# Decoder trunk on one core: the low parts of 40 weight chunks, made by an accumulating DMA instead of a GpSimd subtraction

## The chip, the cores and the metric

The kernel runs on one core of one Trainium2 chip. The metric is device time in microseconds (us), the median of several runs. The profile is one execution taken with the hardware profiler. Engines: PE (TensorE matmuls), PEld (TensorE weight loads), DVE (VectorE), ACT (ScalarE), POOL (GpSimd), SP (SyncE, which issues nearly all DMAs here).

## What is computed

The reference is a decoder trunk of two layers over 512 tokens of width 1024, in float32:

```
for l in range(DEPTH):
    h = rmsnorm(x, attn_norm_w[l])
    proj = h @ w_in[l]                      # split into the inputs of three mixers
    ... y_ssd = ssd_mixer(...); y_sc = short convolution; y_nsa = nsa_mixer(...)
    x = x + concatenate([y_ssd, y_sc, y_nsa]) @ w_out[l]
    h = rmsnorm(x, ffn_norm_w[l])
    u = causal_dwconv(h @ ffn_w_up[l], ffn_conv_w[l], ffn_conv_b[l])
    gate, val = split(u, 2)
    x = x + (silu(gate) * val) @ ffn_w_down[l]
return rmsnorm(x, final_norm_w)
```

## The kernel before, in words

**Products in three parts.** Weights and activations are float32. Each is split into a high part, rounded to the type fp32r, and a low part, the rest. A product is three matmuls into the same PSUM tile (`mul3`, L195 to L200): high weight by high activation (L198), high weight by low activation (L199), low weight by high activation (L200). So the low part of a weight chunk is wanted first by the third matmul of that chunk.

**Weight chunks.** The weights come in chunks of 128x1024 float32 (512 KB), listed in `chunks` (L108 to L128) in the order of their use, each with the engine that makes its low part, V (DVE) or G (POOL). Per layer there are the group chunks, 22 chunks of the input projection mixed with four compression chunks (`w0` to `w3`), 8 of the output projection, and then those of the MLP. G makes 20 whole chunks per layer, 40 in all: 15 of the input projection (q1, xbc2 to xbc7, z0, z2, z3, sc0, sc1, sc3 to sc5) and 5 of the output projection. It also makes two of the compression chunks of a layer, on another path (L172). All chunks of the MLP go to V.

**Staging.** `do_dma` (L132) loads a chunk from HBM into a `raw` tile on the SP queue (3 buffers). `do_prep` (L150) makes the `hl` tile (4 buffers) that holds both parts: ACT copies raw into the high part (L175), which rounds it, and then the chunk's engine subtracts, low = raw - high (L176). `nxt` (L179), called when a chunk's matmuls begin, sees to it that loads are issued to four chunks ahead and chunks prepared to three ahead. An `hl` buffer comes free when PE is done with the chunk four places earlier; a `raw` buffer comes free when both preparing instructions have read it.

**What lies beside it.** In each layer the first part runs the projection and the mixers together: `pull` (L512) inserts steps of the projection between attention and scan pieces. The pieces pass from engine to engine: `scores` (L604) goes PE, DVE, ACT, then scales the probabilities on DVE and POOL (L624); `turn` (L627) transposes on PE (L632), ACT writes the high part (L636), DVE the low part (L639), and `pv` (L646) multiplies on PE (L652). The scan has POOL work at L754, L796, L813, L816 and L817. `post_xbc` (L367) has DVE (L369), ACT (L371), three DVE steps (L373) and an ACT tanh (L374). `values`, `parts` and `post_keys` make operands with ACT and DVE; L334 and L335 belong to `post_q`. The MLP (`ffn`, L934) has no POOL work.

**What sets the order.** Each engine runs its instructions in order, and that order is fixed when the program is built: the framework places instructions on an engine by its own cost estimates and dependencies, while `keep_in_program_order` pins some matmuls behind what was traced before them. Engines wait for one another by semaphores.

Of the kernel before, what the change touches and what calls it, by code (L numbers as in the profile page):

```python
# [10 lines left out]
F32 = mybir.dt.float32  # L11
F32R = mybir.dt.float32r
AF = mybir.ActivationFunctionType
OP = mybir.AluOpType
# [49 lines left out]
def trunk(ctx: ExitStack, tc: tile.TileContext, ins, out):  # L64
    nc = tc.nc
    V, A, G, TE = nc.vector, nc.scalar, nc.gpsimd, nc.tensor
# [7 lines left out]
    def slot(dt=F32, shape=(P, 512)):  # L74
        return ph.tile(list(shape), dt, tag="s", bufs=32, name="s")
# [74 lines left out]
    def do_prep(i):  # L150
        _, w, eng, piece = chunks[i]
        r = raws.pop(i)
        if w < 0:
            ts_ = []
            for j in range(2):
                t = slot(F32R)
                rr = r[:, j * 512:(j + 1) * 512]
                A.activation(t, rr, AF.Copy)
                V.tensor_tensor(t[64:128], rr[64:128], t[64:128].bitcast(F32), op=OP.subtract)
                ts_.append(t)  # L160
            hls[i] = ts_
            return
        t = pw.tile([P, 2, 1024], F32R, tag="hl", bufs=4, name="hl")
        if piece:

            n, line = w // piece, -(-2 * piece // 16) * 16
            t3 = t.rearrange("p e c -> p (e c)")[:, :n * line].rearrange("p (k c) -> p k c", c=line)[:, :, :2 * piece]
            t4 = t3.rearrange("p k (e c) -> p k e c", e=2)
            r3 = r[:, :w].rearrange("p (k c) -> p k c", c=piece)
            for a, b in ((0, 1), (1, 4)) if i == 0 else ((0, n),):  # L170
                A.activation(t4[:, a:b, 0], r3[:, a:b], AF.Copy)
                eng.tensor_tensor(t4[:, a:b, 1], r3[:, a:b], t4[:, a:b, 0].bitcast(F32), op=OP.subtract)  # L172
            hls[i] = t4
            return
        A.activation(t[:, 0, 0:w], r[:, 0:w], AF.Copy)  # L175
        eng.tensor_tensor(t[:, 1, 0:w], r[:, 0:w], t[:, 0, 0:w].bitcast(F32), op=OP.subtract)  # L176
        hls[i] = t

    def nxt():  # L179
        i = st["use"]  # L180
        st["use"] += 1
        while st["dma"] < min(len(chunks), i + 5):
            do_dma(st["dma"])
            st["dma"] += 1
        while st["prep"] < min(len(chunks), i + 4):
            do_prep(st["prep"])
            st["prep"] += 1
        return hls.pop(i)
# [874 lines left out]
    for k in range(KD):  # L1063
        if k in (0, 3, 6):
            do_prep(st["prep"])
            st["prep"] += 1
        n.split(k)
# [109 lines left out]
```

## Time and profile before

| | us |
|---|---|
| median of 3 runs | 1258.81 (1256.79 to 1263.97) |
| the profiled execution's own time | 1256.38 |
| its span, first to last instruction | 1254.6 |
| PE busy / DVE busy / ACT busy / POOL busy | 1199.0 / 879.5 / 581.3 / 226.5 |
| mean granted TensorE clock | 0.988 |

A row of a profile view names the line of the kernel, the engine, the operation and its tiles as out<-in, with partitions x elements and a type. In a timeline a row is the start in us, the duration, the instruction, how many alike follow one another, and in brackets how long the engine had been idle before it and who ended that. In a table by stretch each engine has its busy time in us and its instructions; then come the granted clock (1 is 2.4 GHz, 0.5 is 1.2 GHz), the busy share of the DMA engines and what they moved.

### The profile page before, as it was taken

How to read it: one execution, taken by the hardware profiler on the slowest of the kernel's cores; microseconds unless marked ns; L12 is line 12 of the kernel's file. 1: busy time of each engine (PE TensorE's matmuls, PEld its weight loads, DVE VectorE, ACT ScalarE, POOL GpSimd, SP SyncE). 2: the span in 40 equal slices, each digit the busy share in tenths (PEclk: the TensorE clock that was granted, in tenths of full speed). 3: DMA queues.
4: the chain of work that ended last, by engine and by line, in shares of the span. 5: the costliest groups of instructions: out<-in, count | busy, mean ns of one | idle time of the engine just before them, and what ended most of it. 6: DMA issues, size and time to landing. Idle time of an engine off the chain costs nothing. (4 is left out here: it accounts for less than half of the span.)

```text
span 1254.6 us, 15502 instructions
## 1 busy us (share of the span) xinstructions
PE 1199.0 (96%) x5843; PEld 994.0 (79%) x5843; DVE 879.5 (70%) x1408; ACT 581.3 (46%) x909; POOL 226.5 (18%) x209
## 2 busy tenths in 40 slices
PE   8889899999999999999999888999999999999997
PEld 6767678788888888888877667778888888888897
DVE  6899978567776347775468998795577743677753
ACT  6655554345443224444348455444444421444553
POOL 3443346500000000000043332562000000000001
PEclk9999999999999999999999998999999999999999
DMA  7321123232322332232223211322232333233452
GB/s 257 117 67 51 51 86 100 75 100 95 101 96 90 101 101 98 89 116 91 80 84 101 68 51 51 121 81 84 89 102 95 101 101 95 91 101 101 127 162 99
DMA packets 37051, 121.33 MB, mean 97 GB/s; under 512 B 4144, under 2 KB 6512, under 8 KB 36976
## 3 DMA queue, kind: packets, MB, share of 16 engines
q1 hardware_dynamic: 36832, 120.33, 30.2%
q8 instruction: 46, 0.75, 0.3%
q14 instruction: 29, 0.24, 0.1%
q10 hardware_dynamic: 144, 0.00, 0.0%
HBM read 118.19 MB, written 2.13 MB: 96 GB/s over the span
## 5 line engine op out<-in xcount | busy, mean ns | idle before, releaser
L198 PE MATMUL mm<-h,hl 128*128 128x512 f32 x1040 | 412.3, 396 | 0.8 <-DVE s L369 0.8
L199 PE MATMUL mm<-h,hl 128*128 128x512 f32 x1040 | 408.8, 393 | 0.0
L200 PE MATMUL mm<-h,hl 128*128 128x512 f32 x1040 | 408.6, 393 | 0.1
L175 ACT ACTIVATE hl<-raw 128x1024 fp32r<-128x1024 f32 x198 | 209.6, 1058 | 225.2 <-PE mm L200 122.5
L176 DVE TENSOR_TENSOR hl<-raw,hl 128x1024 fp32r<-128x1024 f32 x158 | 195.5, 1238 | 104.7 <-ACT hl L175 102.6
L198 PEld LDWEIGHTS mm<-h,hl 128*128 128x128 f32 x1040 | 197.3, 190 | 41.0 <-issue 1.0
L200 PEld LDWEIGHTS mm<-h,hl 128*128 128x128 f32 x1040 | 196.7, 189 | 41.1 <-DVE hl L176 0.5
L199 PEld LDWEIGHTS mm<-h,hl 128*128 128x128 f32 x1040 | 197.1, 190 | 39.3
L212 POOL TENSOR_TENSOR m<-m,mhalf 128x1 f32<-128x1 f32 (+2 forms) x14 | 9.9, 708 | 773.7 <-DVE m L211 773.7
L943 DVE SCALAR_TENSOR_TENSOR s<-s,par 128x511 f32<-128x511 f32 (+1 forms) x172 | 128.3, 748 | 3.5 <-ACT s L941 0.6
L176 POOL TENSOR_TENSOR hl<-raw,hl 128x1024 fp32r<-128x1024 f32 x40 | 98.9, 2476 | 123.6 <-ACT hl L175 86.4
L940 DVE TENSOR_TENSOR s<-mm,rstdB 128x512 f32<-128x512 f32 x86 | 59.1, 689 | 66.7 <-PE mm L200 66.7
L199 PE MATMUL mm<-s,hl 128*128 128x512 f32 (+1 forms) x240 | 85.2, 355 | 3.4 <-DVE s L258 3.4
L198 PE MATMUL mm<-s,hl 128*128 128x512 f32 (+1 forms) x240 | 85.5, 357 | 1.1 <-ACT s L257 1.1
L200 PE MATMUL mm<-s,hl 128*128 128x512 f32 (+1 forms) x240 | 85.0, 354 | 0.0
L257 ACT ACTIVATE s<-s 128x512 fp32r<-128x512 f32 (+1 forms) x62 | 33.0, 545 | 111.8 <-DVE s L958 108.0
L198 PE MATMUL aux<-s,hl 128*128 128x512 f32 (+1 forms) x232 | 82.1, 354 | 0.0
L199 PE MATMUL aux<-s,hl 128*128 128x512 f32 (+1 forms) x232 | 81.8, 353 | 0.0
L200 PE MATMUL aux<-s,hl 128*128 128x512 f32 (+1 forms) x232 | 81.8, 353 | 0.0
L941 ACT ACTIVATE s<-s,par 128x512 f32<-128x512 f32 x86 | 69.3, 808 | 8.8 <-DVE s L940 8.2
L258 DVE TENSOR_TENSOR s<-s 128x512 fp32r<-128x512 f32 (+1 forms) x62 | 45.1, 738 | 27.9 <-ACT s L257 27.9
L956 ACT ACTIVATE s<-s 128x512 f32<-128x512 f32 x40 | 25.3, 633 | 78.7 <-DVE s L943 78.7
(257 smaller groups left out, 1677.6 us busy)
## 6 DMA issues: line engine op xcount, KB each, us to landing
raw<-in_w_up SPq DMA_DIRECT2D x86, 512.0 KB, 3.5
raw<-in_w_dn SPq DMA_DIRECT2D x54, 512.0 KB, 3.5
raw<-in_w_in SPq DMA_DIRECT2D x44, 512.0 KB, 3.6
raw<-in_w_out SPq DMA_DIRECT2D x16, 512.0 KB, 3.5
raw<-in_w SPq DMA_DIRECT2D x8, 512.0 KB, 3.5
s<-dr SPq DMA_DIRECT2D x16, 256.0 KB, 4.2
x<-in_xT SPq DMA_DIRECT2D x8, 256.0 KB, 5.8
out<-s SPq DMA_DIRECT2D x8, 256.0 KB, 3.2
```

The source lines that it names most:

```text
L175: A.activation(t[:, 0, 0:w], r[:, 0:w], AF.Copy)
L176: eng.tensor_tensor(t[:, 1, 0:w], r[:, 0:w], t[:, 0, 0:w].bitcast(F32), op=OP.subtract)
L198: TE.matmul(ps, wh, rhs_h, start=first, stop=False)
L199: TE.matmul(ps, wh, rhs_l, start=False, stop=False)
L200: TE.matmul(ps, wl, rhs_h, start=False, stop=last)
L212: G.tensor_tensor(dst, v, mhalf[:, :n], op=OP.pow)
L257: A.activation(dst_h, src, AF.Copy)
L258: V.tensor_tensor(dst_l, src, dst_h.bitcast(F32), op=OP.subtract)
L940: V.tensor_tensor(u, ps, rstdB, op=OP.mult)
L941: A.activation(acc, u, AF.Identity, scale=w[:, 2:3], bias=pr[:, C_FCB + i:C_FCB + i + 1])
L943: V.scalar_tensor_tensor(acc[:, j:], u[:, :T - j], w[:, 2 - j:3 - j], acc[:, j:], op0=OP.mult, op1=OP.add)
L956: A.activation(g, g, AF.Silu)
```

## The change

For the 40 whole chunks of G, ACT writes the negated raw chunk into the low half of the `hl` tile, and a DMA issued on POOL's queue adds the raw chunk to what stands there. The rounding is symmetric, so raw + (-high) is the same low part. V chunks, the compression chunks and the rest are as before.

```
         A.activation(t[:, 0, 0:w], r[:, 0:w], AF.Copy)
-        eng.tensor_tensor(t[:, 1, 0:w], r[:, 0:w], t[:, 0, 0:w].bitcast(F32), op=OP.subtract)
+        if eng is G:
+
+            A.activation(t[:, 1, 0:w], r[:, 0:w], AF.Copy, scale=-1.0)
+            G.dma_start(t[:, 1, 0:w], r[:, 0:w], accum_op=OP.add)
+        else:
+            eng.tensor_tensor(t[:, 1, 0:w], r[:, 0:w], t[:, 0, 0:w].bitcast(F32), op=OP.subtract)
         hls[i] = t
```

## Rows read from the trace of the kernel before

**Rows 1.** The page, first part: PE's busy time, its share, instructions.

```profile
PE 1199.0 (96%) x5843; PEld 994.0 (79%) x5843; DVE 879.5 (70%) x1408; ACT 581.3 (46%) x909; POOL 226.5 (18%) x209
```

**Rows 2.** Table by stretch: layer 0's mixers, layer 1's, two shorter stretches; PE, PEld, DVE, ACT, POOL.

```profile
27.00:250.00 223.00, 200.96 (x1019) 161.03 (x1018) 188.77 (x379) 118.81 (x234) 105.41 (x95) 0.98 0.25 79
...
60.00:90.00 30.00, 23.93 (x112) 18.44 (x111) 27.95 (x61) 16.09 (x34) 13.34 (x8) 0.94 0.29 91
...
636.00:864.00 228.00, 207.78 (x1040) 167.17 (x1040) 187.07 (x378) 122.58 (x236) 104.61 (x94) 0.97 0.25 77
...
690.00:720.00 30.00, 25.35 (x119) 19.87 (x118) 28.06 (x59) 14.78 (x29) 11.29 (x6) 0.94 0.24 71
```

**Rows 3.** Groups: busy us, mean ns of one; idle before, what ended it.

```profile
L175 ACT ACTIVATE hl<-raw 128x1024 fp32r<-128x1024 f32 x198 | 209.6, 1058 | 225.2 <-PE mm L200 122.5 <-PE aux L200 54.5 <-issue 27.7
...
L176 POOL TENSOR_TENSOR hl<-raw,hl 128x1024 fp32r<-128x1024 f32 x40 | 98.9, 2476 | 123.6 <-ACT hl L175 86.4 <-issue 24.2 <-DMA raw<-in_w_in 13.0
```

**Rows 4.** Timeline of layer 0 around 140 us, POOL, DVE and PE.

```profile
137.87 2.42 POOL L176 TENSOR_TENSOR hl<-raw,hl 128x1024 fp32r<-128x1024 f32 x1 [9.22 <-ACT hl L175]
...
138.06 2.87 DVE L624 TENSOR_SCALAR s<-s,m 128x256 f32<-128x256 f32 x2
...
141.73 0.68 DVE L639 TENSOR_TENSOR s<-aux,s 128x512 fp32r<-128x512 f32 x1
...
142.46 0.73 PE L652 MATMUL pv<-s 128*128 128x512 f32 x1 [2.01 <-DVE s L639]
```

**Rows 5.** Timelines of layer 1 around 697 us: POOL, DVE, ACT, PE.

```profile
693.20 5.27 POOL L176 TENSOR_TENSOR hl<-raw,hl 128x1024 fp32r<-128x1024 f32 x2 [3.22 <-ACT hl L175]
...
696.10 2.92 DVE L373 SCALAR_TENSOR_TENSOR s<-s,cwh 128x509 f32<-128x509 f32 x1
...
699.12 0.63 ACT L374 ACTIVATE s<-s 128x512 f32<-128x512 f32 x1 [4.55 <-DVE dtk L689]
...
701.11 0.50 PE L652 MATMUL pv<-s 128*128 128x512 f32 x1 [3.25 <-ACT s L636]
```

**Rows 6.** The instructions of one line, L373: ns least/median/most.

```profile
L373 DVE SCALAR_TENSOR_TENSOR s<-s,cwh x48: 733/744/2925, 81.2 to 760.2; 128x511 f32<-128x511 f32 x16, 128x510 f32<-128x510 f32 x16, 128x509 f32<-128x509 f32 x16
```

**Rows 7.** PE's waits: us in total, times, longest.

```profile
PE pv L652 <- DVE s L639: 12.7, 10, 2.8
...
PE pv L652 <- ACT s L636: 4.2, 2, 3.3
...
PE mm L199 <- DVE s L258: 3.4, 2, 1.7
```

**Rows 8.** PE's timeline: the first and the last of twelve gaps.

```profile
57.91 0.50 PE L611 MATMUL aux<-s 128*128 128x512 f32 x1 [1.22 <-DVE s L335]
...
843.06 0.50 PE L199 MATMUL mm<-s,hl 128*128 128x512 f32 x1 [1.69 <-DVE s L258]
```

**Rows 9.** The raw tiles' loads: from issue to landing.

```profile
DMA to landing us min/median/max: 2.7/3.5/8.5
```

**Rows 10.** Timelines, POOL's then PE's: low parts made and first used.

```profile
27.94 2.39 POOL L176 TENSOR_TENSOR hl<-raw,hl 128x1024 fp32r<-128x1024 f32 x1 [0.55 <-ACT hl L175]
...
38.15 0.39 PE L200 MATMUL mm<-h,hl 128*128 128x512 f32 x1
...
54.92 2.39 POOL L176 TENSOR_TENSOR hl<-raw,hl 128x1024 fp32r<-128x1024 f32 x1 [6.82 <-ACT hl L175]
...
62.20 0.39 PE L200 MATMUL mm<-h,hl 128*128 128x512 f32 x1
...
670.92 2.40 POOL L176 TENSOR_TENSOR hl<-raw,hl 128x1024 fp32r<-128x1024 f32 x1 [12.98 <-DMA raw<-in_w_in]
...
676.55 0.39 PE L200 MATMUL mm<-h,hl 128*128 128x512 f32 x1
```

**Rows 11.** The same for the output projection's last POOL chunk in layer 0.

```profile
246.41 2.40 POOL L176 TENSOR_TENSOR hl<-raw,hl 128x1024 fp32r<-128x1024 f32 x1 [3.21 <-ACT hl L175]
...
261.80 0.39 PE L200 MATMUL mm<-s,hl 128*128 128x512 f32 x1
```

## The prediction, made before the changed kernel ran

> **What bounds the kernel now.** I read the busy shares first, then the table by stretch, then PE's gaps one by one. PE is busy 1199.0 of 1254.6 us [rows 1], so the MLP, where POOL does nothing, leaves nothing to win. The mixers do: there PE is busy 200.96 of 223 us and 207.78 of 228 us [rows 2], which leaves 22.0 + 20.2 = 42 us in gaps, and the change touches these two stretches alone. DVE is the nearly full engine beside PE in them: 27.95 and 28.06 of 30 us in two of the shorter stretches, in both of which the granted clock is 0.94 [rows 2].
>
> Next I asked why DVE is late where PE waits for it. At 137.87 POOL begins a 2.42 us subtraction; DVE's pair L624 begins at 138.06 and takes 2.87 us, ending 0.6 us after POOL; L639 runs at 141.73, and PE's L652 has waited 2.01 us by 142.46 [rows 4]. In layer 1 two subtractions fill 693.20 to 698.47, and a DVE L373 that starts at 696.10 takes 2.92 us [rows 5], where the line's median is 0.744 [rows 6]. ACT, in order, sits 4.55 us behind that DVE work, its L636 comes late, and PE stands 3.25 us [rows 5]. So a DVE instruction that takes its operands from SBUF is **held until POOL's subtraction ends**. DVE instructions that read PSUM (L639, L616, L369) keep their usual time beside POOL.
>
> I followed every PE gap over 0.7 us in the mixers back to such a hold. Twelve begin there: at 57.9, 66.1, 78.7, 84.8, 129.7, 142.5 and 229.2, and at 692.1, 701.1, 741.2, 754.0 and 843.1 (the first and the last stand in [rows 8]). They add up to 21.2 us; the three largest groups of PE's waits, 12.7, 4.2 and 3.4 us [rows 7], are where most of them are booked.
>
> **What is removed.** POOL loses 40 subtractions, 98.9 us [rows 3]. On POOL itself this is worth nothing, as POOL is busy under half of the mixers [rows 2]; the cover is that idle time. What counts is that the twelve gaps lose their cause, at most 21.2 us. With them go slow stretches of the clock: three 30 us stretches (60, 120 and 690 us on; the first and the last in [rows 2]) read 0.94, so 0.06 x 30 = 1.8 us of PE speed each, 5.4 us, each behind one of the large gaps. The upper bound of the gain is 26.6 us, the lower is nothing. I take **two thirds, 17.7 us**: with the hold gone DVE is still the fullest engine beside PE, and some gaps will be taken over by the next DVE or ACT instruction in line.
>
> **What is added on ACT.** 40 copies of 1.058 us [rows 3], 42.3 us, each behind the first copy, so whatever stands behind it on ACT (L636, L334, L271, L618) moves back by 1.06 us. ACT is busy 118.81 of 223 us [rows 2], 53%, so some 22.5 us meet work that is there to be delayed; the rest falls into ACT's idle time, which is its cover. Of the three groups of waits shown, ACT ends 4.2 of 20.3 us [rows 7], 21%. The bounds are 0 and 22.5 us; I take 22.5 x 0.21 = **4.7 us**, nearer to the lower, because most of these waits end with DVE.
>
> **What is added on POOL and the DMA engines.** 40 transfers of a whole chunk inside SBUF, each reading 512 KB twice (raw and what stands in the low half) and writing it once. The trace has no accumulating DMA and none issued on POOL. Call L the time from the end of ACT's second copy to the landing. The nearest row is the raw load: 2.7 least, 3.5 median, 8.5 most [rows 9]. One plain load, 3.5 us, is the lower bound; three passes, 10.5 us, the upper. I take two loads, **L = 7 us**, because two blocks must be read.
>
> Where does a late low part hurt? Before, the subtraction followed the first copy for 2.4 us; now 1.06 + L follow it. So the low part comes later by L - 1.3, with L = 7 by 5.7 us. Counting 24 matmuls to a chunk along PE's timeline gives each of the 40 its slack, from the end of the subtraction to the weight load (0.2 us ahead of the L200 matmul). Three are short: q1 of layer 0 has 38.15 - 30.33 - 0.2 = 7.6 us, xbc2 has 62.20 - 57.31 - 0.2 = 4.7 in layer 0 and 676.55 - 673.32 - 0.2 = 3.0 in layer 1 [rows 10]. The others have 11 us or more; the output projection's last has 261.80 - 248.81 - 0.2 = 12.8 [rows 11]. By 5.7 us xbc2 is late by 1.0 and 2.7 us, **3.7 us** of PE's time; the bounds are 0 (L = 3.5) and 1.6 + 4.5 + 6.2 = 12.3 us (L = 10.5).
>
> The Trainium skill's page "DMA: Bandwidth & Descriptors" (Anatomy of one DMA) fits a DMA issued on GpSimd by about 2.0 us plus its bytes over 436 GB/s. For one pass over 512 KB that is an estimate of 3.2 us, by which no chunk would be late and the sum below would be 13.0 us instead of 9.3. No run here shows such a DMA yet.
>
> POOL's issue now waits for the second copy, 1.06 us later than the subtraction did, and holds back POOL's L624, L754, L813; but the issue should be shorter than the 2.4 us that it replaces, so nothing is added. SP's load of a later chunk needs the raw buffer, which is now free only when the accumulation has landed, 5.7 us later; its chunk is copied three chunks on, so the slack of the output projection (12.8 us) covers it, and if that cover went, each load would cost what exceeds it.
>
> **The sum.** -17.7 + 4.7 + 3.7 = -9.3 us: 1247.1 against the profiled execution's own 1256.38. The median of the runs, 1258.81, stands 2.4 us above that; from it the forecast is **1249.5 us**. What a measurement of this kernel can tell from no change is about 0.5%, 6.3 us.
>
> **The rivals.**
>
> **The port stays taken (0.20).** Issuing on POOL is work too: if GpSimd holds DVE off while it prepares each transfer, the twelve gaps stay in part. For it: a 2.4 us POOL instruction holds DVE [rows 4], and no row shows that issuing is free of this. Against: the issue must last about as long as the subtraction to keep all of them. With no gain the sum is +4.7 + 3.7 = +8.4, 1267; with half of it 1258. About 1262.
> The same page (SWDGE vs HWDGE vs iDMA) says that the descriptor rings of such a DMA lie in SBUF, written by GpSimd, and that VectorE locks GpSimd out there in its two-port mode. No run here shows it yet; it would lengthen L in the stretches where DVE is full.
>
> **Late landing (0.20, slower).** The place is xbc2 in both layers, then q1 of layer 0. With all three late the stall is 3 x (L - 1.3) - 15.3 us. It eats the net gain of 13.0 (17.7 - 4.7) at L = 10.8 us, and passes 0.5% slower at L = 12.9. At L = 15 it is 25.8, with 1 us more per layer in the output projection 27.8: net +14.8, **1273.6**. For it: an accumulation is a kind of transfer that no row prices, and a raw load has taken 8.5 us [rows 9]. Against: the median load takes 3.5, and the DMA engines are busy a quarter of the time [rows 2].
>
> **The change doesn't do what it says (0.10).** The order on each engine is laid anew when the program is built, by estimates that take the new copies and DMAs into account. Pieces that are now back to back may be put elsewhere, so that the gaps move instead of going. Then gain and loss cancel: about 1258.
>
> **How the numbers follow.** The forecast has 0.50; its own range is 1236 (nearly the whole 26.6 us, few costs) to 1258 (L = 10.5). Of it I put 0.45 below the half per cent and 0.05 within. The port rival gives 0.03 faster, 0.11 same and 0.06 slower; late landing 0.01 same and 0.19 slower; the last 0.10 same. So faster 0.48, same 0.27, slower 0.25. The range, from 1236 to 1274, leaves about 0.1 out at each end.
>
> **What would show it.** Right: in the mixers L373 and L624 have no durations over 1.5 us beside a POOL DMA; PE's waits on L639 fall from 12.7 to 4 to 6 us; DVE's busy time in each mixer stretch falls by some 20 us; ACT's rises by 21 per layer; the accumulations land in 5 to 9 us; PE shows one new wait of 1 to 3 us at xbc2 in each layer, released by a DMA. Wrong: PE waiting for a DMA at many chunks (late landing), or DVE instructions still stretched while POOL issues (the port).

## The result, and the profile after

The changed kernel takes **1228.74 us** (median of 4 runs, 1226.1 to 1230.71) against 1258.27 us before (4 runs, 1256.79 to 1263.97): a ratio of 0.976, 95% interval 0.9741 to 0.9778. That is 29.5 us faster, where I had forecast 9.3 us, and it lies below my range. The profiled execution of after took 1227.79 us with a span of 1226.0.

From the page of after, the span, the busy times, and the two DMA queues with their packets, bytes in MB and share (q0 is the one that POOL issues on):

```profile
span 1226.0 us, 15614 instructions
...
PE 1193.8 (97%) x5843; PEld 992.1 (81%) x5843; DVE 827.6 (68%) x1408; ACT 617.3 (50%) x949; POOL 161.6 (13%) x209
...
q1 hardware_dynamic: 36832, 120.33, 31.1%
q0 software_dynamic: 5760, 20.97, 9.0%
```

Read it against [rows 1]. The span is 28.6 us shorter. PE's idle time, span less busy, went from 55.6 to 32.2 us (23.4), and the same 5843 matmuls were 5.2 us quicker. The line to stop at is DVE's: its **same 1408 instructions take 827.6 instead of 879.5 us**, 51.9 us less, although the change touches no DVE instruction.

The table by stretch of after, with the columns of [rows 2]: the first two are the mixers of the two layers, cut so that they hold about the matmuls of the stretches before (1027 and 1036, against 1019 and 1040); the others are the shorter stretches, with the one from 120 that the prediction names.

```profile
27.00:237.00 210.00, 200.48 (x1027) 162.83 (x1026) 163.68 (x381) 137.91 (x256) 72.55 (x94) 0.98 0.53 133
625.00:838.00 213.00, 203.51 (x1036) 164.13 (x1035) 160.66 (x378) 140.76 (x256) 69.65 (x92) 0.98 0.53 131
60.00:90.00 30.00, 26.67 (x129) 21.91 (x128) 24.34 (x70) 23.48 (x44) 6.97 (x8) 0.94 0.63 136
120.00:150.00 30.00, 29.52 (x154) 23.49 (x153) 24.13 (x66) 21.41 (x49) 5.96 (x9) 1.00 0.55 123
690.00:720.00 30.00, 29.07 (x153) 23.02 (x152) 27.98 (x62) 21.08 (x45) 8.07 (x10) 1.00 0.54 136
```

The gain lies where it was looked for. The mixers take 210 and 213 us where they took 223 and 228, which is nearly the whole of it; PE's gaps in them fall from 22.0 and 20.2 to 9.5 and 9.5 us. DVE is busy 25.1 and 26.4 us less, ACT 19.1 and 18.2 us more. The stretches from 120 and 690 read a granted clock of 1.00 instead of 0.94; the one from 60 still reads 0.94. The DMA engines are now busy half of the time instead of a quarter.

The instructions of two lines of after (least/median/most ns), with the landing of what L179 issues; L179 is the accumulating DMA, L378 is L373 of before:

```profile
L179 POOL DMA_DIRECT2D hl<-raw x40: 849/877/1058, 29.8 to 832.5; - x40
...
DMA to landing us min/median/max: 4.5/4.7/8.3
...
L378 DVE SCALAR_TENSOR_TENSOR s<-s,cwh x48: 732/744/1650, 78.2 to 739.2; 128x511 f32<-128x511 f32 x16, 128x510 f32<-128x510 f32 x16, 128x509 f32<-128x509 f32 x16
```

The issue costs POOL 0.88 us in place of 2.4, a landing takes 4.7 us, and the longest L378 is 1.65 us where it was 2.9 [rows 6]. Timelines of after show both cases, a DVE instruction beside the issue of a DMA and one beside arithmetic that POOL still does:

```profile
103.34 1.31 POOL L594 TENSOR_TENSOR s<-s,cst 128x512 f32<-128x512 f32 x1 [0.84 <-ACT ecd L708]
...
103.55 1.65 DVE L378 SCALAR_TENSOR_TENSOR s<-s,cwh 128x510 f32<-128x510 f32 x1
...
126.97 0.85 POOL L179 DMA_DIRECT2D hl<-raw  x1 [6.17 <-ACT hl L178]
...
127.22 0.69 DVE L380 SCALAR_TENSOR_TENSOR s<-s 128x512 f32<-128x512 f32 x1 [0.27 <-ACT s L379]
```

L378 starts at 103.55, POOL's L594 ends at 104.65, and L378 ends 0.55 us after that: the signature of [rows 4], with shorter POOL work. The L380 that starts in the middle of an issue takes 0.69 us, and none of the sixteen L380 takes longer: it isn't held. L375 of before, the same instruction, took up to 2.47 us.

PE's waits of after (us in total, times, longest). L657, L644, L641 and L205 were L652, L639, L636 and L200:

```profile
PE aux L485 <- DVE s L323: 5.2, 2, 3.0
PE aux L637 <- POOL s L629: 3.1, 4, 2.3
PE mm L205 <- DMA hl<-raw: 2.9, 2, 2.0
...
PE pv L657 <- ACT s L641: 1.7, 1, 1.7
...
PE pv L657 <- DVE s L644: 0.7, 2, 0.5
```

The 12.7 us on DVE's low part of the transposed probabilities [rows 7] are 0.7, the 4.2 on ACT are 1.7. The new row is the third, PE waiting for an accumulation. Its two places on PE's timeline are the third matmul of xbc2 in layer 0 and in layer 1:

```profile
62.49 0.50 PE L205 MATMUL mm<-h,hl 128*128 128x512 f32 x1 [0.89 <-DMA hl<-raw]
...
663.79 0.51 PE L205 MATMUL mm<-h,hl 128*128 128x512 f32 x1 [2.03 <-DMA hl<-raw]
```

### The profile page after: what moved, and what is told of

Its sections match the earlier page's. It is cut to its first block, busy times and chain, and to the rows that moved or that the text cites. A ratio compares the mean times of both kernels' runs of the same rounds, so it can differ in the third digit from the quotient of the medians.

```text
span 1226.0 us, 15614 instructions
## 1 busy us (share of the span) xinstructions
PE 1193.8 (97%) x5843; PEld 992.1 (81%) x5843; DVE 827.6 (68%) x1408; ACT 617.3 (50%) x949; POOL 161.6 (13%) x209
## 5 line engine op out<-in xcount | busy, mean ns | idle before, releaser
L205 PE MATMUL mm<-h,hl 128*128 128x512 f32 x1040 | 408.4, 393 | 3.0 <-DMA hl<-raw 2.9
L205 PEld LDWEIGHTS mm<-h,hl 128*128 128x128 f32 x1040 | 196.3, 189 | 44.8 <-DMA hl<-raw 3.8
L205 PE MATMUL mm<-s,hl 128*128 128x512 f32 (+1 forms) x240 | 84.9, 354 | 0.0
L205 PE MATMUL aux<-s,hl 128*128 128x512 f32 (+1 forms) x232 | 81.8, 353 | 0.0
L263 DVE TENSOR_TENSOR s<-s 128x512 fp32r<-128x512 f32 (+1 forms) x62 | 36.2, 595 | 28.4 <-ACT s L262 28.4
L179 POOL DMA_DIRECT2D hl<-raw x40 | 35.1, 878 | 133.9 <-ACT hl L178 101.4
```

What stands on the lines that cost most here:

```text
L179: G.dma_start(t[:, 1, 0:w], r[:, 0:w], accum_op=OP.add)
L205: TE.matmul(ps, wl, rhs_h, start=False, stop=last)
L263: V.tensor_tensor(dst_l, src, dst_h.bitcast(F32), op=OP.subtract)
```

## The experiments

My theory after the result: a DVE instruction that takes its operands from SBUF is held by POOL's subtraction, and the mixers lose nearly the whole held time, not only the gaps that I could trace. The first rival: the order on each engine is laid anew in the changed program, and the better order is the gain. The second: the DMA engines doing the work is what counts, not DVE's release. All times are medians of 4 runs, with the ratio to runs of before on the same chip. Three chips were used, and the medians of before on them are 1258.3, 1258.6 and 1259.4 us, so a difference between kernels that ran on different chips carries about 1 us.

**The sum back on POOL.** The changed kernel, but POOL adds, instead of the DMA:

```
-            G.dma_start(t[:, 1, 0:w], r[:, 0:w], accum_op=OP.add)
+            G.tensor_tensor(t[:, 1, 0:w], r[:, 0:w], t[:, 1, 0:w].bitcast(F32), op=OP.add)
```

> The changed kernel with POOL adding the raw chunk to the negated high part in place of the DMA; the values are the same, and the order of the instructions on each engine is nearly that of the changed kernel. Port theory (POOL's two-operand instruction holds VectorE's SBUF work, the DMA does not): the 28 us come back almost whole, 1250 to 1262 us, DVE's busy time rises by 35 to 55 us over the changed kernel's 827.6, and L378 shows durations over 2 us beside POOL again. Order theory (the gain is the new order that the build lays out): it stays at 1226 to 1236 us. Half and half: about 1243.

1270.61 us, ratio 1.0083 (1.0068 to 1.0098), above both ranges that I had written down. Its order is nearly that of after (of PE's 5843 matmuls the first 3030 are the same, and 77 of the later places differ), yet it is 41.9 us slower than after. The busy times, and L378 and L179:

```profile
PE 1208.3 (95%) x5843; PEld 998.1 (79%) x5843; DVE 878.5 (69%) x1408; ACT 616.9 (49%) x949; POOL 223.7 (18%) x209
...
L378 DVE SCALAR_TENSOR_TENSOR s<-s,cwh x48: 732/744/2927, 83.0 to 775.8; 128x511 f32<-128x511 f32 x16, 128x510 f32<-128x510 f32 x16, 128x509 f32<-128x509 f32 x16
...
L179 POOL TENSOR_TENSOR hl<-raw,hl x40: 2351/2397/3095, 29.4 to 874.4; 128x1024 fp32r<-128x1024 f32 x40
```

DVE is back at 878.5 us, L378 at 2.9 us: the hold is back, and the gain is gone. The new order, with ACT's copies in it, gives nothing. What this kernel has over before, the second copy on ACT, a later start of the POOL work and the new order, costs 12.3 us together (11.2 against before on the same chip).

**A plain transfer.** The changed kernel without the accumulation, so that the raw chunk itself stands in the low half:

```
-            G.dma_start(t[:, 1, 0:w], r[:, 0:w], accum_op=OP.add)
+            G.dma_start(t[:, 1, 0:w], r[:, 0:w])
```

> The changed kernel with a plain DMA in place of the accumulating one, so the low part is the raw chunk instead of raw minus high; the order on every engine is that of the changed kernel. If accumulating lengthens the transfer by its second read, the landing falls from 4.7 us to 3.5 to 4, the two waits at xbc2 (0.9 and 2.0 us) shrink by about that, and the time falls by 0 to 3 us: 1226 to 1229. If accumulating costs nothing, landing 4.5 to 4.8 and 1228 to 1230.

1220.64 us, ratio 0.9692 (0.9673 to 0.9712), 5.4 us below my range. Every engine runs the instructions of after in the order of after, so the 8.1 us between them are the accumulation, but for what other values in the low half may do to PE, which no run separates. Its busy times, DMA rows and wait:

```profile
PE 1190.4 (98%) x5843; PEld 990.5 (81%) x5843; DVE 826.1 (68%) x1408; ACT 616.3 (51%) x949; POOL 150.1 (12%) x209
...
q0 software_dynamic: 5760, 20.97, 4.9%
...
L179 POOL DMA_DIRECT2D hl<-raw x40: 527/576/771, 29.8 to 825.7; - x40
...
DMA to landing us min/median/max: 2.9/3.0/5.2
...
PE mm L205 <- DMA hl<-raw: 0.6, 2, 0.3
```

The same bytes take 4.9% of the DMA engines instead of 9.0%, land in 3.0 us instead of 4.7, and the wait at xbc2 shrinks from 2.9 to 0.6 us. PE's busy time is 3.4 us less as well, at a mean granted clock of 0.993 instead of 0.990. Between this kernel and the one before, DVE's busy time falls by 52.4 us and the time by 50.0.

**A copy on POOL instead.** POOL has a short instruction with one operand; it too leaves the raw chunk in the low half:

```
-            G.dma_start(t[:, 1, 0:w], r[:, 0:w], accum_op=OP.add)
+            G.tensor_copy(t[:, 1, 0:w], r[:, 0:w])
```

> The changed kernel with POOL copying the raw chunk into the low half (one operand) in place of the DMA, so the low part is the raw chunk; the order on each engine is that of the run in which POOL adds. If any POOL work on SBUF holds VectorE for as long as it lasts, the copy, which should take 1 to 1.5 us instead of 2.4, gives back half of what the adding cost: 1240 to 1258 us. If only two-operand POOL work holds it: 1226 to 1234.

1230.01 us, ratio 0.9763 (0.9741 to 0.9784). PE, DVE and ACT run exactly the order of the sum on POOL. Only POOL's instruction is 1.04 us instead of 2.40:

```profile
PE 1194.0 (97%) x5843; PEld 990.1 (81%) x5843; DVE 838.1 (68%) x1408; ACT 616.8 (50%) x949; POOL 170.1 (14%) x209
...
L179 POOL CAST hl<-raw x40: 1032/1042/1482, 30.9 to 834.2; 128x1024 fp32r<-128x1024 f32 x40
```

DVE is busy **40.4 us less, and the kernel is 40.6 us faster**, with no DMA in it. The second rival falls with this. Beside the plain transfer, DVE has 12.0 us more and the kernel 9.4: a copy of one operand holds DVE too, for its shorter time. The 1230 us lie in the range that I had given to the other reading, that only POOL work with two operands holds; I had overpriced the copy. The next count decides between them.

**The held time, counted.** Take every DVE instruction that runs beside POOL's whole-chunk work, and count what it takes beyond the usual time of its line and shape (the lower quartile over all runs), where that is over 0.2 us. In before 38 instructions are held for 53 us, the longest for 2.2 us; with the sum on POOL 40 for 53 us; beside the copy 22 for 12 us, 0.85 at most; in after and with the plain transfer one each for under 0.5 us, and POOL's L629 runs beside it, too. So nearly all of DVE's 51.9 us is held time. What after keeps, some 27 us, lies beside POOL's other arithmetic.

**The subtraction in quarters.** The kernel before, with nothing moved:

```
-        eng.tensor_tensor(t[:, 1, 0:w], r[:, 0:w], t[:, 0, 0:w].bitcast(F32), op=OP.subtract)
+        n = 4 if eng is G else 1
+        for q in range(n):
+            c = slice(q * w // n, (q + 1) * w // n)
+            eng.tensor_tensor(t[:, 1, c], r[:, c], t[:, 0, c].bitcast(F32), op=OP.subtract)
```

> The kernel before with each of POOL's 40 subtractions cut into four of 256 columns; the order on PE, DVE and ACT is exactly that of the kernel before. Port theory: a held VectorE instruction waits for the quarter in progress, some 0.6 us, instead of up to 2.4, so its excess falls from about 50 us to 15 to 25, and the time falls with it, to 1225 to 1242 us. If the hold lasts until POOL has nothing left to do, or if the order was what mattered: 1255 to 1266.

1236.41 us, ratio 0.9823 (0.9796 to 0.9851), with PE, DVE and ACT in exactly the order of before:

```profile
PE 1198.0 (97%) x5843; PEld 992.5 (80%) x5843; DVE 858.1 (69%) x1408; ACT 581.0 (47%) x909; POOL 259.0 (21%) x329
...
L179 POOL TENSOR_TENSOR hl<-raw,hl x160: 719/739/1209, 28.7 to 846.8; 128x256 fp32r<-128x256 f32 x160
...
L376 DVE SCALAR_TENSOR_TENSOR s<-s,cwh x48: 733/750/1328, 81.5 to 749.5; 128x511 f32<-128x511 f32 x16, 128x510 f32<-128x510 f32 x16, 128x509 f32<-128x509 f32 x16
```

POOL is busy 32.5 us more, DVE 21.4 us less [rows 1], and the kernel is 21.9 us faster: a held DVE instruction now waits for the end of a quarter (0.74 us) only. By the same count 70 instructions are held for 32 us, none for over 0.6 us. So the hold is shown in the kernel before itself, without the DMA and without a new order.

**All 40 on DVE.** The kernel before, with POOL's whole chunks given to V:

```
-                chunks.append((ins["w_in"][l, TILES.index(nm)], 1024, G if PLAN["eng"][ORDER.index(nm)] else V, 0))
+                chunks.append((ins["w_in"][l, TILES.index(nm)], 1024, V, 0))
...
-            chunks.append((ins["w_out"][l, i], 1024, G if PLAN["engo"][i] else V, 0))
+            chunks.append((ins["w_out"][l, i], 1024, V, 0))
```

> The kernel before with the 40 subtractions on VectorE. Port theory: VectorE gains 40 x 1.23 = 49 us of work and loses the holds, which cost it about as much, so the time stays within 8 us of before, 1250 to 1266. If the holds were cheap (the twelve gaps alone, 21 us, and the rest covered), it is slower by 15 to 40 us, 1273 to 1298.

1233.73 us, ratio 0.979 (0.9775 to 0.9805), faster than either of my ranges. Its busy times:

```profile
PE 1192.4 (97%) x5843; PEld 990.9 (80%) x5843; DVE 871.2 (71%) x1448; ACT 581.2 (47%) x909; POOL 132.5 (11%) x169
```

DVE does 40 instructions more, 1.24 us each and 50 us in all, and is busy 8.3 us **less**. What POOL took off DVE's hands cost DVE more than doing it. The order is its own, so the time is not the hold's alone.

**Source order on every engine**, for before and for after (`keep_in_program_order` on every instruction of the four engines), meant to compare the two in one order:

```
-    V, A, G, TE = nc.vector, nc.scalar, nc.gpsimd, nc.tensor
+    class Pin:
+
+        def __init__(self, e):
+            self.e = e
+
+        def __getattr__(self, what):
+            f = getattr(self.e, what)
+            return lambda *a, **k: tc.keep_in_program_order(f(*a, **k))
+
+    V, A, G, TE = Pin(nc.vector), Pin(nc.scalar), Pin(nc.gpsimd), Pin(nc.tensor)
```

> The kernel before with every instruction of the four compute engines kept in the order of the source, so that the build lays out no order of its own. It is a base for the next run; slower than before by 0 to 80 us by either theory.

> The changed kernel with every instruction of the four compute engines kept in the order of the source. Port theory: faster than the kernel before in the same fixed order by 15 to 40 us. Order theory: within 6 us of it, or slower by the cost of the copies on ACT.

1471.01 us (ratio 1.1673, 1.1655 to 1.169) and 1468.09 us (1.1659, 1.1634 to 1.1685): no difference clear of the noise, and both far over the 80 us that I had allowed for. The busy times of the first, whose span is 1468.1, and of the second, 1464.7:

```profile
PE 1269.3 (86%) x5843; PEld 1034.9 (70%) x5843; DVE 859.8 (59%) x1408; ACT 577.8 (39%) x909; POOL 222.8 (15%) x209
...
PE 1263.5 (86%) x5843; PEld 1029.2 (70%) x5843; DVE 843.0 (58%) x1408; ACT 613.9 (42%) x949; POOL 160.8 (11%) x209
```

PE is idle 198.8 us here and 201.2 in the other, so in this order other waits set the time, and DVE, busy 59% of it, gives 16.8 us (859.8 against 843.0) that are worth nothing that could be measured. By what I had written down, a difference of under 6 us spoke for the order theory. It doesn't carry that: the kernels with equal orders above contradict it. What it does show is that DVE's lost time has its price only where DVE is nearly full beside PE.

**Without the second copy.** The plain transfer, and ACT's L178 taken out:

```
-            A.activation(t[:, 1, 0:w], r[:, 0:w], AF.Copy, scale=-1.0)
```

> As the run with the plain DMA, and without ACT's second copy: the low part is the raw chunk, moved by a plain DMA that waits for the raw load alone. It leaves out the 40 negated copies, and the build lays out its own order. If the copies cost the 4.7 us of the forecast: 1221 to 1226 us, of which up to 3 are the waits at xbc2. If they lie in ACT's idle time: 1225 to 1230.

1215.89 us, ratio 0.9654 (0.9631 to 0.9677), below both of my ranges and 4.75 us below the plain transfer, where ACT's copies take 41.9 us. Its order is its own (713 of PE's 5843 places differ), and its transfers needn't wait for a copy, so this holds the copies and what their absence does to both.

**Which chunks.** Four kernels keep the change and deal the chunks out otherwise. The first gives the DMA xbc0, xbc1, z1, sc2 and the whole output projection, and DVE xbc2:

```
-    'eng': [0, 0, 0, 1, 1, 1, 0, 0, 0, 0, 1, 1, 1, 1, 1, 1, 1, 0, 1, 1, 1, 1, 0, 1, 1, 1],
-    'engo': [0, 1, 0, 1, 1, 1, 1, 0],
+    'eng': [0, 0, 0, 1, 1, 1, 1, 0, 1, 0, 0, 1, 1, 1, 1, 1, 1, 1, 1, 1, 1, 1, 1, 1, 1, 1],
+    'engo': [1, 1, 1, 1, 1, 1, 1, 1],
```

> The change on more chunks of the mixers: xbc0, xbc1, z1, sc2 and all of the output projection go to POOL's DMA, xbc2, whose low part came late, to VectorE. VectorE loses 12 more subtractions of 1.23 us. If VectorE still limits the mixers: 1218 to 1226 us. If what is left of PE's gaps has other causes (POOL's other work, the compression chunks): within 3 us of the changed kernel, 1226 to 1232.

The second gives DVE xbc2 and the two compression chunks that POOL still subtracted:

```
-    'eng': [0, 0, 0, 1, 1, 1, 0, 0, 0, 0, 1, 1, 1, 1, 1, 1, 1, 0, 1, 1, 1, 1, 0, 1, 1, 1],
+    'eng': [0, 0, 0, 0, 1, 0, 0, 0, 0, 0, 0, 1, 1, 1, 1, 1, 1, 0, 1, 1, 1, 1, 0, 1, 1, 1],
```

> The changed kernel with xbc2, whose low part came late by DMA (2.9 us of PE's waits), and the two compression chunks that POOL still subtracts on VectorE. Port theory: the DMA waits go and two more holds per layer with them, for 1.2 us of VectorE each: 1219 to 1226 us. If nothing is left to gain there: 1226 to 1232.

The third adds z1, sc2 and the whole output projection, which have slack, to the second:

```
-    'eng': [0, 0, 0, 0, 1, 0, 0, 0, 0, 0, 0, 1, 1, 1, 1, 1, 1, 0, 1, 1, 1, 1, 0, 1, 1, 1],
-    'engo': [0, 1, 0, 1, 1, 1, 1, 0],
+    'eng': [0, 0, 0, 0, 1, 0, 0, 0, 0, 0, 0, 1, 1, 1, 1, 1, 1, 1, 1, 1, 1, 1, 1, 1, 1, 1],
+    'engo': [1, 1, 1, 1, 1, 1, 1, 1],
```

> As the run with the tight chunks on VectorE, and z1, sc2 and all of the output projection by the accumulating DMA. VectorE loses 10 subtractions of 1.23 us: if it still limits the mixers, 1212 to 1222 us; if the rest of PE's gaps has other causes, within 3 us of the run with the tight chunks alone.

The fourth makes the compression chunks' low parts by the DMA, too:

```
-                eng.tensor_tensor(t4[:, a:b, 1], r3[:, a:b], t4[:, a:b, 0].bitcast(F32), op=OP.subtract)
+                if eng is G:
+                    A.activation(t4[:, a:b, 1], r3[:, a:b], AF.Copy, scale=-1.0)
+                    G.dma_start(t4[:, a:b, 1], r3[:, a:b], accum_op=OP.add)
+                else:
+                    eng.tensor_tensor(t4[:, a:b, 1], r3[:, a:b], t4[:, a:b, 0].bitcast(F32), op=OP.subtract)
```

> The changed kernel with the two compression chunks of POOL in each layer made by the accumulating DMA too. Port theory: two holds per layer go, worth up to 2 us each, but w1 has little time before its use in layer 1, where a landing of 5 us or more comes late: 1223 to 1231 us. If their DMA, in runs of 512 bytes, is slow: 1230 to 1240.

| chunks | us | ratio (95%) |
|---|---|---|
| as the change has them | 1228.74 | 0.976 (0.9741 to 0.9778) |
| more by DMA, xbc2 on DVE | 1232.18 | 0.979 (0.9762 to 0.9819) |
| xbc2, w0, w1 on DVE | **1223.39** | 0.9705 (0.9677 to 0.9733) |
| the same, those with slack by DMA | 1231.4 | 0.9777 (0.9754 to 0.98) |
| compression by DMA too | 1226.7 | 0.9739 (0.9717 to 0.9761) |

The kernel with xbc2, w0 and w1 on DVE is the fastest that computes the whole: 34.9 us below before, as I had expected. It has no wait of PE for a DMA. The first and the third missed the gain that I expected if DVE still limits the mixers. Their PE waits tell why more chunks by DMA are no better; first the one with more by DMA, then the one with the slack chunks:

```profile
PE aux L795 <- DVE s L775: 7.4, 3, 4.2
PE mm L205 <- DMA hl<-raw: 6.8, 3, 5.7
```

```profile
PE aux L795 <- DVE s L775: 8.5, 4, 3.1
```

xbc0, wanted early, is late by 5.7 us in layer 0, and xbc1 by 0.95 in layer 1. In both kernels a scan step waits 7 to 9 us for DVE's L775 where after has 1.8 us. That is a hold again, by the scan's own POOL work. The kernel with the slack chunks has the first two rows, after the third:

```profile
196.11 5.63 DVE L775 TENSOR_TENSOR s<-s,dte 128x512 f32<-128x512 f32 x1
...
199.88 1.30 POOL L801 TENSOR_TENSOR s<-s,ecd 128x512 f32<-128x512 f32 x1
...
195.45 1.12 DVE L775 TENSOR_TENSOR s<-s,dte 128x512 f32<-128x512 f32 x1
```

L775 ends 0.56 us after the last of five POOL instructions that begin at 196.30 and follow one another without a pause. The new order has put them side by side. In the kernel with xbc2, w0 and w1 on DVE this wait is 1.0 us; the 7.5 us more are nearly the 8.0 us by which the slack chunks made the kernel slower. The kernel with the compression chunks by DMA can't be told from after: PE waits 5 us in all for its new transfers.

## Why the prediction was right about the sign and wrong about the size

**The mechanism: right.** POOL's subtraction holds DVE instructions that take their operands from SBUF until it ends, and the change ends the hold: L378 falls from 2.9 to 1.65 us at most, with the rest beside other POOL arithmetic; the quarters show it in the kernel before, in which nothing else is moved. The Trainium skill's page "SBUF — State Buffer" (Who interferes with whom) has it that GpSimd and VectorE share a port pair that one instruction locks for its whole length, and that a VectorE instruction with two SBUF inputs meets a GpSimd instruction that reads SBUF. The trace agrees, in length (2.9, 1.65 and 1.33 us for L373 beside 2.4, 1.31 and 0.74 us of POOL) and in that the copy of one operand holds too.

**The gain, "two thirds, 17.7 us" of "at most 21.2 us" plus 5.4 of clock: the step that failed.** I took as a bound the twelve PE gaps over 0.7 us that I could follow back to a hold, and discounted that for gaps that "will be taken over by the next DVE or ACT instruction in line". Both halves were wrong. Little was taken over: the waits on L644 and L641 fell to 0.7 and 1.7 us, and only PE's wait for POOL's L629, L624 of before, grew, from 1.4 us to 3.1:

```profile
PE aux L632 <- POOL s L624: 1.4, 3, 0.8
```

And gaps were the wrong thing to count: the net gain of 29.5 us, with all costs in it, is larger than the bound of 26.6. I had the held time nearly right. My own sign was that "DVE's busy time in each mixer stretch falls by some 20 us"; measured are 25.1 and 26.4. What failed is its price: DVE, at 28 of 30 us, was nearly as full as PE, and most of what it lost came back as time, also where I could trace no gap. Where the order on PE, DVE and ACT is equal or nearly so, the kernel follows DVE's time closely:

| from, to | DVE busy, us | time, us |
|---|---|---|
| subtraction whole, in quarters (same order) | -21.4 | -21.9 |
| sum on POOL, copy on POOL (same order) | -40.4 | -40.6 |
| sum on POOL, plain transfer | -52.4 | -50.0 |
| copy on POOL, plain transfer | -12.0 | -9.4 |

DVE's time is that of the profiled executions, the kernel's the median of its runs. The profiled execution of the quarters took 1240.74 us, 4.3 above its median, and that of before 1256.38. Profiled against profiled the four times are -15.6, -39.9, -49.1 and -9.2 us. So a microsecond of DVE's was worth 0.7 to 1.0 of the kernel's.

So the gross gain was about 50 us, and my upper bound of 26.6 was half of it. From the sum on POOL to the plain transfer PE's idle time falls by 31.2 us (59.7 to 28.5) and its busy time by 17.9 us, at a mean granted clock of 0.993 instead of 0.982; my 21.2 and 5.4 were too small in both. The steps from before to after are +12.3 (copies, later start, order), -50.0 (DVE released) and +8.1 us (accumulation). They meet the 29.5 us of the result because each starts where the last one ended, so their sum proves nothing. With ACT's copies at 4.75 us instead of the 12.3, the gross gain would be 42.4 us; no run separates the 7.6 us between the two.

**ACT's copies, 4.7 us: near, but not shown.** The one measurement gives 4.75, in another order, so that the two agree to 0.1 us is luck. The term also took each copy to stand "behind the first copy"; in 22 of the 40 chunks ACT does other work between the two. That they add 18 to 19 us to ACT's busy time in each layer's mixers, where I said 21, is nearly as forecast.

**Landing and xbc2, L = 7 and 3.7 us: right in place, near in size by luck.** The landing is 4.7 us after the issue (4.5 to 8.3), between one load and two. The two waits come where the slack rows [rows 10] put them, 0.89 and 2.03 us where I had 1.0 and 2.7. But L at xbc2, from the end of the second copy, was 5.4 and 5.2 us, and with that my sum gives 0 and 0.9. The rest lies on ACT. In layer 1 four other ACT instructions stand between the two copies of xbc2:

```profile
653.83 1.06 ACT L175 ACTIVATE hl<-raw 128x1024 fp32r<-128x1024 f32 x1
...
657.50 1.06 ACT L178 ACTIVATE hl<-raw 128x1024 fp32r<-128x1024 f32 x1
```

The second begins 2.6 us after the first has ended. In layer 0 the copies adjoin, but the first begins at 55.05 instead of 53.78, while PE is ready at 61.60 instead of 62.20. Too long an L and too much slack made up for one another.

By the estimate from the Trainium skill's page "DMA: Bandwidth & Descriptors" (Anatomy of one DMA), 3.2 us, no wait would have come. That figure fits the plain transfer (3.0 us measured), whose two waits are 0.6 us together; the accumulating one takes 1.7 us more. What I missed is that it costs 8.1 us, not 3.7: beside 2.3 us of waits there are 3.4 us of PE's busy time, at the lower clock, and 2.4 us that I can't place.

**POOL's and SP's queues, nothing: nearly.** SP now waits for the accumulations before it loads into a raw buffer, as I had it, and ACT's waits for raw loads, 1.4 us in two before, are 4.5 us in three after. From ACT's waits of after:

```profile
ACT hl L175 <- DMA raw<-in_w_in: 4.5, 3, 3.0
```

PE shows no wait that ends with these copies; what the 3 us do beyond ACT I did not follow.

**The rivals.** The port doesn't stay taken: accumulation and plain transfer differ by 0.30 us in each of 40 issues, 12 us, and by 1.5 us in DVE's busy time; 40 copies of 1.04 us make it 12.0. The Trainium skill's page "SBUF — State Buffer" (SBUF: two separate sides) warns that GpSimd can't write a DMA's descriptors while VectorE has the port in a two-port mode; no issue of a whole chunk took over 1.06 us here, so no run here shows such a wait in the issue. The longest landing, 8.3 us, is that of an accumulation in flight together with the next one and with raw loads; what lengthened it I did not separate. Late landing stayed at two waits, 2.9 us. That the order would eat the gain is refuted by the result; it can account for some of the 12.3 us against the change, at most.

## What to carry to other kernels

Where instructions of one engine hold those of another, compare the busy time of the held engine with its usual durations, instruction by instruction. If that engine is nearly full beside the bounding one, most of the loss is the price (0.7 to 1.0 of it here), not only the gaps that can be traced to it; where other waits set the time, as in source order, it can be worth nothing. An engine that is "free" may cost more than it takes over: giving POOL's 40 subtractions to DVE itself made DVE's total shorter. When work goes to a DMA, keep the pieces that are wanted soonest on an engine, and look in the new order for what now stands beside the holding engine.

## What the runs showed of the hardware that I had not expected

- Cutting a POOL instruction in four makes POOL slower (259.0 instead of 226.5 us busy) and the kernel 21.9 us faster: the length of the single instruction is what DVE waits for (2.2 us at most beside a whole one, 0.6 beside quarters).
- An accumulating transfer of 512 KB inside SBUF lands 4.7 us after its issue and a plain one 3.0; POOL is busy 0.88 and 0.58 us with the issue; the share of the DMA engines is 9.0% against 4.9%. So adding to the destination, instead of overwriting it, makes the landing 1.6 times as long.
- Issuing such DMAs on POOL leaves DVE's instructions at their usual time, although POOL is busy for nearly as long as with a copy that does hold them (0.88 and 1.04 us).
